# RWKV chunk in a hybrid token-mixer kernel: the key and value products ordered over all four quarters of TensorE

## The chip, the cores and the metric

One Trainium2 chip, one of its eight NeuronCores. The time is device microseconds of one execution of the whole program, which is a single launch. Before the change three runs took 4097.76, 4099.77 and 4100.25 us; the median is 4099.77 us.

## The reference

The reference is a two-layer block of a flow-matching generator over 1024 latent tokens and 256 context tokens of width 1024. Each layer normalises, projects by `w_in`, runs three groups of recurrent heads (RetNet retention, gated linear attention, RWKV-7), joins them in one output projection and ends with a SwiGLU feed-forward part. Every scan runs forward and backward. The part that matters here is the RWKV-7 scan with six heads of width 64:

```python
def _rwkv_scan(seq, s0):
    """S_t = S_{t-1}(diag(w_t) - kk_t^T (kk_t a_t)) + v_t^T k_t, o_t = S_t r_t."""
    def step(s, inp):
        rt, wt, kt, vt, kkt, at = inp
        sa = jnp.einsum("bhvk,bhk->bhv", s, -kkt)
        s = s * wt[:, :, None, :] + sa[..., None] * (kkt * at)[:, :, None, :] + vt[..., None] * kt[:, :, None, :]
        return s, jnp.einsum("bhvk,bhk->bhv", s, rt)
...
o_c, o_l = _bidirectional(_rwkv_scan, _rwkv_scan, cf, cb, lf, lb, s0)
```

## The kernel before, in words

The scan is done in chunks of 64 tokens. `rwkv` makes 20 steps in each layer, and a step holds one forward and one backward chunk (d = 0, 1). For each step `pre(u)` prepares what does not need the state and runs two steps ahead, and `step(u)` does the recurrence. In layer 0 all 20 steps give an output; in layer 1 the four context steps give none, so 36 steps of the 40 have the full set of products.

Six heads are three pairs j with two halves e: half e lies on partitions 64e to 64e+63 of `AR` (decayed queries and erase keys) and `BK` (keys). In `pre` the products of `AR` and `BK` are made by the code of lines 1282 to 1307. For half e there are first products, six matmuls 128 columns wide, whose result is masked by VectorE into `SA` (one instruction) and `SR` (two), and second products, six matmuls 64 columns wide, masked into `SR` by two more. A half's rows sit on one 64-row half of the array; the two directions d go to its two 64-column halves. So a half uses two quarters of the array, and the two halves use the other two each.

All these results go to PSUM tiles with the tag `d`, of which there are two (`self.pr("d", 2)`). The same two hold the block products of `XE` and `Wc` (32 by 32) that come just ahead in `pre`, and the transposes of `BK` that follow (line 1314, evicted to `BKT`). A tile is reused when its readers are done.

In the profile `rd` is a PSUM tile of that tag, `ra`, `rs` and `rb` are the PSUM tiles of `step`, `pd` are the dense products of the input projections of the gated linear attention and the retention (`gla_in`, `ret_in`), and `gvs`, `gkhT` are operands of the state update of the gated linear attention. Nearly all matmuls have line 245 (`mm`), since one helper issues them; the masks have line 640. An f32 matmul of the program is two matmul instructions in the trace, so six make 12.

What sets the order: the program is not run in the order of the code. `TileContext(nc, schedule_with_timeline_sim=True)` reorders the instructions of each engine by a planned timeline; `tc.high_priority` puts `step` and `pre` ahead (`HP = 5000,4500,4500`), and `run` feeds the dense products of `gla_in` and `ret_in` between the steps by a budget (`DT`, `N1`, `N2`). TensorE takes its instructions in the order so planned.

Of the kernel before, what the change touches and what calls it, by code (L numbers as in the profile page):

```python
# [16 lines left out]
D = 1024  # L17
# [21 lines left out]
SR = 0  # L39
# [131 lines left out]
class Kern:  # L171
# [287 lines left out]
    def rwkv_in(self, l, V, W1, xh, xl, ctx_out):  # L459
# [27 lines left out]
        def col(ct, wh, wl, c0, full, rows=128):  # L487
# [17 lines left out]
            c = self.t(p, [128, PW], "c", bufs=4)  # L505
            R = slice(0, rows)
            tp = V["taps"]
            self.act(c[R], u[R, 1:PW + 1], AF.Copy, scale=tp[R, 1, ct:ct + 1])
            nc.vector.scalar_tensor_tensor(c[R], u[R, 0:PW], tp[R, 0, ct:ct + 1], c[R], op0=ALU.mult, op1=ALU.add)
            nc.vector.scalar_tensor_tensor(c[R], u[R, 2:PW + 2], tp[R, 2, ct:ct + 1], c[R], op0=ALU.mult, op1=ALU.add)  # L510
            return c
# [169 lines left out]
    def rw_inverses(self, l, p):  # L681
# [3 lines left out]
        for u in range(20):  # L685
# [9 lines left out]
            for e in range(2):  # L695
                R = slice(64 * e, 64 * e + 64)
                ps = self.pn()
                for j in range(3):
                    for d in range(2):
                        a, k = M[R, d, j, 0:64], M[R, d, j, 64:128]  # L700
                        self.mm(ps[64 * d:64 * d + 64, 64 * j:64 * j + 64], *((a, k) if d else (k, a)))
# [531 lines left out]
    def rwkv(self, l, V, ctx_out):  # L1233
# [3 lines left out]
        mA, mK, mB = (self.rwmask[:, 64 * i:64 * i + 64] for i in (1, 2, 3))  # L1237
# [6 lines left out]
        D = range(2)  # L1244
        heads, masked, where = self.rw_heads, self.rw_masked, rw_where

        def pre(u):
            out = ctx_out or u >= 4
# [3 lines left out]
            AR = self.t(p, [128, 2, 3, 128], "AR", bufs=NB)  # L1252
            BK = self.t(p, [128, 2, 3, 128], "BK", bufs=2)
# [17 lines left out]
            ps = self.pr("d", 2)  # L1271
# [10 lines left out]
            SA = self.t(p, [128, 6, 64], "SA", bufs=NB)  # L1282
            SR = self.t(p, [128, 2, 6, 64], "SR", bufs=NB) if out else None
            n = 128 if out else 64
            for e in range(2):
                R = slice(64 * e, 64 * e + 64)
                ps = self.pr("d", 2)
                pv = ps[:, 0:384].rearrange("p (j x) -> p j x", j=3)
                for j in range(3):
                    for d in D:  # L1290
                        q = 64 - 64 * d
                        self.mm(pv[q:q + 64, j, 0:n], BK[R, d, j, q:q + 64], AR[R, d, j, 0:n])
                masked(heads(SA, e), pv[:, :, 0:64], mA)
                if not out:
                    continue
                for d in D:
                    q = slice(64 - 64 * d, 128 - 64 * d)
                    masked(heads(SR[q, d], e), pv[q, :, 64:128], mK[q])
                ps = self.pr("d", 2)
                pv = ps[:, 0:192].rearrange("p (j x) -> p j x", j=3)  # L1300
                for j in range(3):
                    for d in D:
                        q = 64 * d
                        self.mm(pv[q:q + 64, j], BK[R, d, j, q:q + 64], AR[R, d, j, 64:128])
                for d in D:
                    q = slice(64 * d, 64 * d + 64)
                    masked(heads(SR[q, d], e), pv[q], mB[q])
            nc.vector.tensor_tensor(BK.rearrange("p d j x -> p (d j) x"), BK.rearrange("p d j x -> p (d j) x"),
                                    PC.rearrange("p d j -> p (d j)").unsqueeze(2).to_broadcast([128, 6, 128]), op=ALU.mult)
            BKT = self.t(p, [128, 2, 384], "BKT", bufs=NB)  # L1310
            for d in D:
                ps = self.pr("d", 2)
# [67 lines left out]
        with hp(1):  # L1380
            cur = [pre(u) for u in range(2)]
        yield
        for u in range(20):
            with hp(0):
                step(u, cur[u])
            if u + 2 < 20:
                with hp(1):
                    cur.append(pre(u + 2))
            yield
# [574 lines left out]
```

## Time and profile before

| what | value |
|---|---|
| median of 3 runs | 4099.77 us |
| the profiled execution, its own time | 4102.32 us |
| its span, first to last instruction | 4100.5 us |
| granted TensorE clock, mean of the span | 0.959 |
| TensorE matmul busy | 3765.7 us, 92% of the span |
| VectorE busy | 2590.2 us, 63% |
| ScalarE busy | 1755.4 us, 43% |
| GpSimd busy | 1507.7 us, 37% |

The span and the time of the profiled execution differ by 1.8 us, which lies around the instructions; that execution was 2.5 us above the median. The page cuts the span into 40 slices of 102.5 us. The products of the change lie between 347 and about 745 us (layer 0) and between about 2495 and 2876 us (layer 1). Matmuls are pipelined: a row's length is from its start to the end of its last result, so what a group occupies on TensorE is read from its start to the start of the next group.

### The profile page before, as it was taken

How to read it: one execution, taken by the hardware profiler on the slowest of the kernel's cores; microseconds unless marked ns; L12 is line 12 of the kernel's file. 1: busy time of each engine (PE TensorE's matmuls, PEld its weight loads, DVE VectorE, ACT ScalarE, POOL GpSimd, SP SyncE). 2: the span in 40 equal slices, each digit the busy share in tenths (PEclk: the TensorE clock that was granted, in tenths of full speed). 3: DMA queues.
4: the chain of work that ended last, by engine and by line, in shares of the span. 5: the costliest groups of instructions: out<-in, count | busy, mean ns of one | idle time of the engine just before them, and what ended most of it. 6: DMA issues, size and time to landing. Idle time of an engine off the chain costs nothing. (4 is left out here: it accounts for less than half of the span.)

```text
span 4100.5 us, 78165 instructions
## 1 busy us (share of the span) xinstructions
PE 3765.7 (92%) x30344; PEld 3125.4 (76%) x30344; DVE 2590.2 (63%) x4602; ACT 1755.4 (43%) x3538; POOL 1507.7 (37%) x1670
## 2 busy tenths in 40 slices
PE   7998999889998999999994997999889988999998
PEld 4776888776677988888883675887766768999886
DVE  3565657657846766665765464667657578556666
ACT  5442334234436744443524443344234465344442
POOL 1155640333435823224331145740323443222443
PEclk9998999999999999999996998999989999999999
DMA  7487545655516522125421387555754232222542
GB/s 225 110 238 187 134 124 156 179 178 186 174 64 215 185 75 93 72 82 211 140 88 57 95 229 203 136 145 142 203 183 143 91 133 98 83 75 97 186 163 103
DMA packets 624771, 582.55 MB, mean 142 GB/s; under 512 B 315276, under 2 KB 517264, under 8 KB 607504
## 3 DMA queue, kind: packets, MB, share of 16 engines
q1 hardware_dynamic: 624112, 576.50, 46.1%
q8 instruction: 240, 3.93, 0.4%
q0 software_dynamic: 288, 1.05, 0.1%
q14 instruction: 131, 1.07, 0.1%
HBM read 431.14 MB, written 146.28 MB: 141 GB/s over the span
## 5 line engine op out<-in xcount | busy, mean ns | idle before, releaser
L1456 POOL TENSOR_TENSOR slo<-raw,shi 128x512 fp32r<-128x512 f32 x467 | 668.2, 1446 | 1084.0 <-ACT shi L1455 996.4
L1455 ACT CAST shi<-raw 128x512 fp32r<-128x512 f32 x478 | 293.7, 621 | 495.0 <-PE pd L245 199.6
L1736 DVE TENSOR_TENSOR f<-pm,f 128x512 f32<-128x512 f32 (+1 forms) x400 | 252.1, 635 | 167.9 <-PE pm L245 164.4
L245 PE MATMUL pm<-hh,shi 128*128 128x512 f32 (+1 forms) x880 | 327.7, 373 | 8.5 <-ACT hh L1722 5.3
L439 POOL TENSOR_TENSOR wlo<-wraw,whi 128x512 fp32r<-128x512 f32 x120 | 167.7, 1407 | 440.7 <-ACT whi L438 439.8
L245 PE MATMUL pm<-hl,shi 128*128 128x512 f32 (+1 forms) x880 | 326.3, 371 | 0.3 <-DVE hl L1723 0.3
L245 PE MATMUL pm<-hh,slo 128*128 128x512 f32 (+1 forms) x880 | 325.0, 369 | 0.0
L245 PE MATMUL pd<-whi,xh 128*128 128x256 f32 x1072 | 314.7, 294 | 2.7 <-DVE st L443 2.7
L245 PE MATMUL pd<-wlo,xh 128*128 128x256 f32 x1072 | 314.1, 293 | 0.5 <-POOL wlo L439 0.5
L245 PE MATMUL pd<-whi,xl 128*128 128x256 f32 x1072 | 314.0, 293 | 0.0
L245 PE MATMUL pd<-xh,whi 128*128 128x512 f32 (+1 forms) x720 | 270.8, 376 | 17.6 <-DVE xl L383 12.0
L245 PE MATMUL pd<-xl,whi 128*128 128x512 f32 (+1 forms) x720 | 272.1, 379 | 3.4 <-DVE xl L383 3.1
L245 PE MATMUL pd<-xh,wlo 128*128 128x512 f32 (+1 forms) x720 | 268.5, 373 | 0.9 <-POOL wlo L439 0.9
L1455 ACT CAST shi<-tw 128x512 fp32r<-128x512 f32 x200 | 123.5, 620 | 303.5 <-PE pd L245 230.9
L245 PEld LDWEIGHTS pd<-whi,xh 128*128 128x128 f32 x1072 | 209.5, 196 | 10.4 <-DVE st L443 3.3
L245 PEld LDWEIGHTS pd<-wlo,xh 128*128 128x128 f32 x1072 | 210.2, 196 | 7.9 <-issue 5.4
L245 PEld LDWEIGHTS pd<-whi,xl 128*128 128x128 f32 x1072 | 210.1, 196 | 6.7 <-issue 4.7
L245 PEld LDWEIGHTS pm<-hh,shi 128*128 128x128 f32 x880 | 166.2, 189 | 42.8 <-DVE f L1736 6.9
L245 PEld LDWEIGHTS pm<-hl,shi 128*128 128x128 f32 x880 | 166.7, 189 | 29.6 <-DVE hl L1723 1.4
L245 PEld LDWEIGHTS pm<-hh,slo 128*128 128x128 f32 x880 | 166.4, 189 | 28.4
L1456 DVE TENSOR_TENSOR slo<-tw,shi 128x512 fp32r<-128x512 f32 x200 | 143.5, 718 | 64.9 <-ACT shi L1455 64.8
L245 PEld LDWEIGHTS pd<-xh,whi 128*128 128x128 f32 x720 | 140.1, 195 | 49.1 <-DVE xl L383 13.5
(402 smaller groups left out, 10905.8 us busy)
## 6 DMA issues: line engine op xcount, KB each, us to landing
raw<-in_wgu SPq DMA_DIRECT2D x72, 1024.0 KB
wmod<-in_w_mod SPq DMA_DIRECT2D x192, 256.0 KB
raw<-in_wd SPq DMA_DIRECT2D x44, 1024.0 KB
wraw<-in_w_in SPq DMA_DIRECT2D x100, 256.0 KB
a<-ops SPq DMA_DIRECT2D x80, 288.0 KB
h<-h SPq DMA_DIRECT2D x44, 512.0 KB
h<-u SPq DMA_DIRECT2D x19, 1024.0 KB
X<-ops SPq DMA_DIRECT2D x36, 480.0 KB
```

What stands on the lines that cost most here:

```text
L245: return self.nc.tensor.matmul(out, l, r, start=start, stop=stop, skip_group_check=skip)
L439: nc.gpsimd.tensor_tensor(wl[i][:, :, w], r, wh[i][:, :, w].bitcast(F32), op=ALU.subtract)
L1455: self.nc.scalar.copy(hi, src)
L1456: e.tensor_tensor(lo, src, hi.bitcast(F32), op=ALU.subtract)
L1736: nc.vector.tensor_tensor(facc[b][:, m, :], ps, facc[b][:, m, :], op=ALU.add)
```

## The change: what it does

The loop over the halves e moves inside. A new inner function `halves` takes a PSUM tile of tag `d` for each half and issues, for each pair j, the products of both halves and both directions, which lie on the four 64 by 64 quarters of the array. First products of both halves are issued first, then the masks, then the second products of both halves. The numbers of matmuls, masks and PSUM tiles stay what they were.

```diff
             n = 128 if out else 64
-            for e in range(2):
-                R = slice(64 * e, 64 * e + 64)
-                ps = self.pr("d", 2)
-                pv = ps[:, 0:384].rearrange("p (j x) -> p j x", j=3)
+            E = range(2)
+
+            def halves(width, x0, swap):
+
+                pv = [self.pr("d", 2)[:, 0:3 * width].rearrange("p (j x) -> p j x", j=3) for _ in E]
                 for j in range(3):
+                    for e in E:
+                        for d in D:
+                            R, q = slice(64 * e, 64 * e + 64), 64 - 64 * d if swap else 64 * d
+                            self.mm(pv[e][q:q + 64, j, 0:width], BK[R, d, j, q:q + 64], AR[R, d, j, x0:x0 + width])
+                return pv
+            pv = halves(n, 0, True)
+            for e in E:
+                masked(heads(SA, e), pv[e][:, :, 0:64], mA)
+            if out:
+                for e in E:
                     for d in D:
-                        q = 64 - 64 * d
-                        self.mm(pv[q:q + 64, j, 0:n], BK[R, d, j, q:q + 64], AR[R, d, j, 0:n])
-                masked(heads(SA, e), pv[:, :, 0:64], mA)
-                if not out:
-                    continue
-                for d in D:
-                    q = slice(64 - 64 * d, 128 - 64 * d)
-                    masked(heads(SR[q, d], e), pv[q, :, 64:128], mK[q])
-                ps = self.pr("d", 2)
-                pv = ps[:, 0:192].rearrange("p (j x) -> p j x", j=3)
-                for j in range(3):
+                        q = slice(64 - 64 * d, 128 - 64 * d)
+                        masked(heads(SR[q, d], e), pv[e][q, :, 64:128], mK[q])
+                pv = halves(64, 64, False)
+                for e in E:
                     for d in D:
-                        q = 64 * d
-                        self.mm(pv[q:q + 64, j], BK[R, d, j, q:q + 64], AR[R, d, j, 64:128])
-                for d in D:
-                    q = slice(64 * d, 64 * d + 64)
-                    masked(heads(SR[q, d], e), pv[q], mB[q])
+                        q = slice(64 * d, 64 * d + 64)
+                        masked(heads(SR[q, d], e), pv[e][q], mB[q])
```

The planned order moves with it. On TensorE, in the third step of layer 0 (its queries are `AR_3494`, its keys `BK_3495`), this is the difference at the last products of `pre`; `ra` belongs to the recurrence of the same step, and lines with - are the order before:

```order
 L245 MATMUL pd_4175<-whi_731_3802,xl_111_316 128x256
-L245 MATMUL rd_3563<-AR_3494,BK_3495 64x128 x6
-L245 MATMUL rd_3573<-AR_3494,BK_3495 64x64 x6
 L245 MATMUL pd_4175<-whi_732_3803,xh_110_315 128x256
 L245 MATMUL pd_4175<-wlo_734_3805,xh_110_315 128x256
 L245 MATMUL pd_4175<-whi_732_3803,xl_111_316 128x256
+L245 MATMUL rd_3564<-AR_3494,BK_3495 64x64 x6
+L245 MATMUL ra_5215<-SAV_3506,SA_3542 64x64 x2
+L245 MATMUL rd_3565<-AR_3494,BK_3495 64x64 x6
+L245 MATMUL ra_5215<-SAV_3506,SA_3542 64x64 x8
+L245 MATMUL ra_5215<-SD_647_3199,AR_3494 64x128 x6
```

Before, the second half's first and second products (`rd_3563`, `rd_3573`) stood together here; now the second products of both halves (`rd_3564`, `rd_3565`) do, and the recurrence's products `ra` stand among them and behind, in one stretch.

Further up in the same step, on TensorE in the order after the change, the first products of one half (`rd_3544`) stand behind the block products `rd_3513` and six of `rs`, and those of the other half (`rd_3545`) do not follow them:

```order
L245 MATMUL rs_4044<-SD_646_3198,AR_3321 64x128 x6
L245 MATMUL rd_3513<-XE_3509 32x32 x12
L245 MATMUL rd_3544<-AR_3494,BK_3495 64x128 x6
L245 MATMUL pd_3962<-whi_731_3802,xh_108_313 128x256
L245 MATMUL pd_3962<-wlo_733_3804,xh_108_313 128x256
...
L245 MATMUL rd_3513<-Wc_3512,XE_3509 32x32
L245 MATMUL rd_3545<-AR_3494,BK_3495 64x128 x6
L245 MATMUL ra_5215<-SAV_3506,SA_3542 64x64 x2
```

The tile of `rd_3545` is the one that `rd_3513` holds until its second round is evicted, so 18 dense products and the second round of the block products lie between the two halves' first products.

One more place, on TensorE before the change, where the gated linear attention updates its state with two chunk halves in two PSUM tiles (the rows of `gvs` and `gkhT` of `pd_5480` lie on the first 64 partitions, those of `pd_5488` on the other 64):

```order
L245 MATMUL pd_5420<-whi_908_5401,xl_107_312 128x256
L245 MATMUL rd_7714<-AR_7645,BK_7646 64x128 x6
L245 MATMUL pd_5480<-gvs_5458,gkhT_5477 64x96 x4
L245 MATMUL pd_5488<-gvs_5458,gkhT_5477 64x96 x4
L245 MATMUL rd_7724<-AR_7645,BK_7646 64x64 x6
L245 MATMUL pd_5681<-whi_907_5400,xh_106_311 128x256
```

The change leaves these products as they are. All four of the one row half stand ahead of all four of the other.

## Rows read from the trace of the kernel before

**Rows 1.** The page: span, and busy time of each engine

```profile
span 4100.5 us, 78165 instructions
PE 3765.7 (92%) x30344; PEld 3125.4 (76%) x30344; DVE 2590.2 (63%) x4602; ACT 1755.4 (43%) x3538; POOL 1507.7 (37%) x1670
```

**Rows 2.** Windows: busy time in the two stretches that hold the scan

```profile
core 0: us, PE busy (x) PEld busy (x) DVE busy (x) ACT busy (x) POOL busy (x), PEclk, DMA share, GB/s
345.00:745.00 400.00, 378.58 (x5671) 327.89 (x5672) 249.29 (x574) 149.86 (x428) 151.41 (x250) 0.97 0.53 138
2495.00:2890.00 395.00, 369.92 (x5535) 318.70 (x5536) 254.96 (x563) 156.70 (x451) 169.57 (x280) 0.98 0.56 146
```

**Rows 3.** Waits of TensorE, 345 to 745 us: sum, times, longest

```profile
PE rs L245 <- ACT R L1333: 7.9, 4, 4.5
PE rd L245 <- DVE SR L640: 2.9, 4, 1.2
...
PE rd L1314 <- DVE BK L1308: 1.3, 2, 1.0
```

**Rows 4.** Waits of TensorE, 2495 to 2890 us

```profile
PE rd L245 <- DVE SR L640: 4.5, 4, 2.3
PE ra L245 <- DVE SA L640: 1.9, 2, 1.0
```

**Rows 5.** Groups by form, whole span: the products that the change orders

```profile
L245 PE MATMUL rd<-AR,BK 64*64 64x128 f32 x864 | 64.6, 282 | 3.7 <-ACT XE L1281 3.7
L245 PE MATMUL rd<-AR,BK 64*64 64x64 f32 x960 | 44.8, 224 | 7.4 <-DVE SR L640 7.4
```

**Rows 6.** Timeline of TensorE at 638 us: start, length, group

```profile
637.99 0.87 PE L245 MATMUL rd<-AR,BK 64*64 64x128 f32 x12 [1.09 <-ACT XE L1281]
638.70 0.57 PE L245 MATMUL pd<-gvs,gkhT 64*64 64x96 f32 x16
639.03 0.51 PE L245 MATMUL rd<-AR,BK 64*64 64x64 f32 x12
639.47 0.39 PE L245 MATMUL pd<-whi,xh 128*128 128x256 f32 x1
...
640.26 0.80 PE L245 MATMUL ra<-SAV,SA 64*64 64x64 f32 x20
640.99 0.88 PE L245 MATMUL ra<-SD,AR 128*64 128x128 f32 x12
```

**Rows 7.** Timeline of TensorE at 357 us

```profile
356.96 0.28 PE L245 MATMUL pd<-wlo,xh 128*128 128x256 f32 x1
357.08 0.28 PE L245 MATMUL pd<-whi,xl 128*128 128x256 f32 x1
357.29 0.87 PE L245 MATMUL rd<-AR,BK 64*64 64x128 f32 x12
359.20 0.56 PE L245 MATMUL rd<-AR,BK 64*64 64x64 f32 x12 [1.03 <-DVE SR L640]
```

**Rows 8.** Timeline of TensorE at 386 us (12 of 128 and 12 of 64 columns)

```profile
385.95 1.22 PE L245 MATMUL rd<-AR,BK 64*64 64x128 f32 x24
387.10 0.38 PE L245 MATMUL pd<-whi,xl 128*128 128x256 f32 x1
```

**Rows 9.** Timeline of VectorE at 358 us: masks behind the key products

```profile
355.09 1.44 DVE L1257 TENSOR_TENSOR BK<-X 128x192 f32<-128x192 f32 x1
356.45 1.97 DVE L1258 TENSOR_TENSOR BK<-X 128x192 f32<-128x192 f32 x1
358.34 0.71 DVE L640 TENSOR_TENSOR SR<-rd,rwmask 64x192 f32<-64x192 f32 x2
359.08 0.36 DVE L640 TENSOR_TENSOR SA<-rd,rwmask 128x192 f32<-128x192 f32 x1
359.47 0.72 DVE L640 TENSOR_TENSOR SR<-rd,rwmask 64x192 f32<-64x192 f32 x2
```

**Rows 10.** Tile SR: masks, ns min/median/max; then who waited, us, times

```profile
L640 DVE TENSOR_TENSOR SR<-rd,rwmask x288: 336/356/364, 352.4 to 2877.1; 64x192 f32<-64x192 f32 x144
...
PE rd L245: 7.4, 8
```

## The prediction

> **What bounds the kernel now.** I read the page first: matmuls are busy for 3765.7 of 4100.5 us, and no other engine comes near [rows 1]. A share over the whole span does not say what the scan is worth, so the second view was the busy time by windows around the two stretches that hold the products of the change. There TensorE is busy for 378.58 of 400 us and 369.92 of 395 us, VectorE for 249 and 255 [rows 2]. TensorE stands for 21.4 and 25.1 us, 46.5 us in both. So the scan is bound by TensorE's own work: the recurrence is covered by dense products that the planner puts between its links, and a microsecond of TensorE time saved there is a microsecond off the stage, as long as no new wait eats it. What comes after the stage is moved forward as a whole: the later parts start when this stage gives back its pools.
>
> The third view was the waits of TensorE. On the masks of `SR` it waited 2.9 us in four places in layer 0 and 4.5 us in four in layer 1 [rows 3, 4]; the tile view gives the same 7.4 us over eight [rows 10]. The largest other one here is `rs` on the copy `R`, 7.9 us [rows 3]. The key products are 864 instructions of 128 columns and 960 of 64 [rows 5]: 36 steps of 24 and 24, and four steps with 24 of 64.
>
> **What a group of products costs now.** Within a half, two quarters already work at once. The 12 instructions of 128 columns occupy TensorE from 637.99 to 638.70, 0.71 us; the 12 of 64 columns from 639.03 to 639.47, 0.44 us, with the way out to the full array [rows 6]. Without that way out the 64-column group is the difference of two rows: 24 instructions with both widths last 1.22 us [rows 8], the 12 wide ones alone 0.87 [rows 7], so 0.35 us.
>
> Do the two row halves run side by side when they stand together? The state update of the gated linear attention answers it: 16 instructions of 96 columns, eight on each row half in PSUM tiles of their own, go from 638.70 to 639.03, 0.33 us [rows 6]. At the rate of one row half (0.71 / 12 = 0.059 us for 128 columns, 0.044 for 96) they would take 16 x 0.044 = 0.71 us. So four quarters do it in half the time, although in the order all of one half stand ahead of all of the other. The order within a stretch matters little; that both halves are in one stretch matters.
>
> A rule speaks against this. The Trainium skill, "TensorE: Matmul & The Clock Gate", "Part 3: Packing small matmuls — row/col tiling", says that matmuls start and end strictly in program order and only weight loads are pulled ahead; in the section "Wait — 56ns, not 53.3ns?" it says that start-to-start never drops below about 25 ns however small the matmul. By the first, two halves that follow each other would not overlap at all and the gain on the second products would be nothing; by the second, an estimate from that page, 24 instructions of 64 columns would take at least 24 x 0.025 = 0.60 us against 0.70 now, so 0.10 us a step and not 0.35. The state update took 0.33 / 16 = 21 ns an instruction, out of order by halves; the trace disagrees with both here.
>
> **The change part by part.** Matmuls, masks, transposes and PSUM tiles keep their numbers. What moves is who stands with whom.
>
> First products (128 columns). The code issues both halves alternately, but the planned order has the two halves' first products in one stretch in 0 of 36 steps, as before: one half takes the free `d` tile, the other waits for the tile of the block products and stands 18 dense rows later. Gain 0. Were they together it would be 0.71 - 12 x 0.004 us, about 0.7 us a step, 25 us in all; that is the upper end and a rival.
>
> Second products (64 columns). Before, both halves share a stretch in 0 of 36 steps; after, in 27. Each saves one group: 27 x 0.35 = 9.5 us. Lower end 0 (no overlap), upper end 36 x 0.35 = 12.6. That the products of `ra` stand among them costs nothing: they use the same 64 by 64 shape.
>
> Changes of shape. I call a stretch a run of matmuls in the order that use the array in one tile shape. Entering a small shape from the full array costs 0.21 us from start to start where dense rows stand 0.12 apart, 0.09 more [rows 7]; leaving costs the 0.44 - 0.35 = 0.09 of above. Between small shapes: 20 instructions of `ra` take 640.26 to 640.99, 0.73 us, of which 20 x 0.35 / 12 = 0.58 is streaming, so 0.15 for way in and out together [rows 6]. I take 0.15 us a stretch. The order has 363 stretches before and 315 after from the first to the last `rd` of layer 0, and 358 and 322 in layer 1; behind layer 1's scan it has 242 and 256, and elsewhere none more or less. Net 48 + 36 - 14 = 70 fewer, 70 x 0.15 = 10.5 us. Ends: 0, if these switches lie beside waits anyway, and 70 x 0.18 = 12.6. Part of this is the planner's luck and not the change's idea: now the second products of both halves ride with `ra`.
>
> Waits. A step's masks do not change in number or price: `SA` 0.36 us, two of `SR` 0.71 [rows 9]. Before, the second half's first products needed the tile that three masks of the first half had to leave, which is the 1.03 us wait at 359.20 and the like [rows 7, 10]. After, second products need tiles that three masks a half must leave, six masks or 2.1 us in a row, and the order puts 15 to 18 dense rows (1.8 to 2.2 us at 0.12) between the second half's first products and the second products. So the old wait of 7.4 us can go, and one of the same kind can come. Behind the waiting matmul stand the second products, `ra` of the recurrence and the dense products, all of TensorE. I take 0; the ends are 7.4 us gained and 36 x 1.03 = 37 us lost.
>
> Sum: 9.5 + 10.5 = 20 us less. The profiled execution took 4102.3 us, 1.8 of it around the span; 4102.3 - 20 = 4082.3, and the median of the runs is 2.5 below that execution: 4079.8, say 4080.
>
> **The rivals.**
>
> 1. More than that: the masks' wait goes (7.4), `ra` also fits beside, and stage waits shrink: 4080 - 7.4 - 5 = 4068 and below; with the first products side by side as well 4055. For it: the halves' streams are independent in the state update. Against: 0 of 36 in the order. Chance 0.08.
>
> 2. No difference to be told: the halves do not overlap on the key products as they did on the state update (a tile's wait stands between them, or `ra` holds the queue), so 9.5 becomes 0 to 3, and half of the switches were beside waits: 4099.8 - 3 - 5 = 4092, and a microsecond or two of new waits puts it at 4093 to 4106. For it: the planner's order is new in the whole stage, and the 46.5 us that TensorE stands there [rows 2] can move by some us either way. Chance 0.20. The Trainium skill's rule of strict program order, named above, would lead here. The variant in which the change does not do what it says belongs here: it already holds for the first products.
>
> 3. Slower: the second products wait on the six masks of both tiles. VectorE is behind where its key products are long (1.44 and 1.97 us just ahead of the masks [rows 9]), and now both tiles hang on it at once, so nothing of `pre` can start. At the 1.03 us of row 359.20 in each of 36 steps this costs 37 us: 4080 + 37 = 4117. It beats the gain from the point where waits of `rd` on the masks grow by more than 20 us, so past 27 us in all against 7.4. Against it: 1.8 to 2.2 us of dense products stand ahead in most steps. Chance 0.12.
>
> **How the numbers follow.** The forecast, 4080 with its own range 4068 to 4091, has 0.60. What a measurement can tell from no change is about 0.2%, 8.2 us: faster is below 4091.6, slower above 4108.0. Faster 0.60 + 0.08 = 0.68, same 0.20, slower 0.12. The range 4060 to 4102 leaves out the far part of rival 1 (0.02), the upper part of rival 2 (0.05) and rival 3 (0.12).
>
> **What would show it.** In the profile after: groups of the key products of 64 columns keep x960 but their union of busy time falls from 44.8 us, while the 128-column ones stay near 64.6 [rows 5]; a timeline row of both halves' second products goes in about 0.35 us for 24 instructions; the stage's busy time of TensorE is 8 to 12 us less a layer, with standing time about as now. Wrong would be: 24 second products that take 0.7 us (no overlap); waits of `rd` on the masks over 20 us; or the same busy time and a shifted stage end, which would say that the stage was not bound by TensorE.

## The result, and the profile after

The changed kernel is slower: 4125.67 us median of four runs (4116.6 to 4132.05), against 4098.77 (4094.44 to 4100.25) for the kernel before on the same chip. The ratio is 1.0062, with a 95% interval of 1.0039 to 1.0085. The prediction said 4080 us; its sign is wrong. The profiled execution of the changed kernel took 4116.6 us, the lowest of its four runs, so the traces account for 14 us and the medians for 27. Most of what is missing goes with the clock: that execution had a granted clock of 0.955, the other three, of 4125.5 to 4132.1 us, 0.950 to 0.952. Over all repeated runs here a run is some 2.8 us longer where its clock is 0.001 lower than its kernel's mean (an estimate by a straight line), so 0.0035 less is worth about 10 us.

The page, span and busy times; the rows of before are [rows 1]:

```profile
span 4114.8 us, 78164 instructions
PE 3757.8 (91%) x30344; PEld 3118.0 (76%) x30344; DVE 2606.3 (63%) x4602; ACT 1757.5 (43%) x3538; POOL 1504.5 (37%) x1670
```

TensorE is busy for 7.9 us less and the span is 14.3 us longer. The windows around the two scans, against [rows 2]:

```profile
core 0: us, PE busy (x) PEld busy (x) DVE busy (x) ACT busy (x) POOL busy (x), PEclk, DMA share, GB/s
345.00:745.00 400.00, 370.11 (x5682) 323.25 (x5683) 256.57 (x573) 150.68 (x429) 152.73 (x253) 0.96 0.53 137
2495.00:2890.00 395.00, 361.37 (x5449) 313.28 (x5450) 247.36 (x554) 155.80 (x443) 167.64 (x282) 0.94 0.55 145
```

Busy time fell by 8.5 us in each window, inside the predicted 8 to 12. In windows of a fixed length standing time (time in which TensorE does nothing) then rises by as much, from 21.4 to 29.9 and from 25.1 to 33.6 us, and the second window holds 86 matmuls fewer; so the windows alone do not say what was gained. The granted clock went from 0.97 and 0.98 to 0.96 and 0.94. The groups by form over the whole span, against [rows 5]:

```profile
L245 PE MATMUL rd<-AR,BK 64*64 64x128 f32 x864 | 63.7, 279 | 3.5 <-DVE SR L640 3.4
...
L245 PE MATMUL ra<-SAV,SA 64*64 64x64 f32 x960 | 51.8, 230 | 13.7 <-DVE SA L640 12.8
...
L245 PE MATMUL rd<-AR,BK 64*64 64x64 f32 x960 | 42.3, 235 | 3.7 <-ACT XE L1281 3.6
```

The busy time of the 64-column products fell from 44.8 to 42.3 us only, less than the sign that the prediction gave. Their instructions now stand among those of `ra`, and such rows overlap; what they occupy is read from starts, below. The wait of `rd` on the masks of `SR`, which rival 3 was about, fell from 7.4 to 3.4 us. TensorE waits elsewhere now: first the rows for 345 to 745 us, then those for 2495 to 2890 us (sum, times, longest), against [rows 3, 4]:

```profile
PE rs L245 <- ACT R L1334: 10.9, 8, 4.0
PE ra L245 <- DVE SA L640: 7.9, 5, 2.8
...
PE rd L245 <- DVE SR L640: 0.4, 2, 0.2
```

```profile
PE rs L245 <- ACT R L1334: 13.5, 4, 7.4
...
PE ra L245 <- DVE SA L640: 4.9, 7, 1.8
PE rd L245 <- DVE SR L640: 3.0, 7, 0.5
```

Before, TensorE did not wait for `SA` in layer 0, and for `R` in layer 1 only this long:

```profile
PE rs L245 <- ACT R L1333: 1.6, 3, 1.0
```

So the waits for `R` went from 9.5 to 24.4 us, those for `SA` from 1.9 to 12.8, those for `SR` from 7.4 to 3.4: 21.8 us more.

The overlap of the two halves is seen at 537.74 us on TensorE's timeline:

```profile
537.74 0.57 PE L245 MATMUL rd<-AR,BK 64*64 64x64 f32 x22
538.24 0.38 PE L245 MATMUL pd<-xh,whi 128*128 128x256 f32 x1
```

22 of the 24 instructions of both halves' second products occupy TensorE for 0.50 us; 12 of one half alone took 0.44 with the way out [rows 6]. So the four quarters do work side by side. The Trainium skill, "TensorE: Matmul & The Clock Gate", in "Wait — 56ns, not 53.3ns?", has a floor of about 25 ns from start to start; here it is 0.50 / 22 = 23 ns with the way out included, and the measurement decides.

**Where the time went, stretch by stretch.** I cut the two layers where the scan begins (first `rd`), where it ends (last product of `step`) and where the last dense product of the input projections stands. Before, then after, scan and rest in turn for layer 0 and layer 1:

```profile
346.60:745.50 398.90, 378.41 (x5676) 328.16 (x5678) 247.69 (x572) 149.86 (x428) 149.97 (x248) 0.97 0.52 138
745.50:880.80 135.30, 112.68 (x907) 106.65 (x903) 77.25 (x198) 31.39 (x75) 46.54 (x52) 0.91 0.62 180
2515.20:2885.80 370.60, 353.03 (x5401) 304.70 (x5403) 242.83 (x537) 146.39 (x421) 149.38 (x245) 0.99 0.56 145
2885.80:2994.20 108.40, 91.72 (x758) 87.23 (x754) 68.63 (x178) 23.27 (x56) 46.13 (x59) 0.97 0.70 204
```

```profile
346.00:741.60 395.60, 367.19 (x5648) 320.83 (x5650) 254.49 (x568) 149.93 (x427) 151.81 (x252) 0.96 0.52 137
741.60:876.00 134.40, 116.06 (x934) 109.27 (x931) 79.30 (x202) 30.81 (x76) 45.05 (x50) 0.90 0.64 186
2516.10:2891.60 375.50, 348.07 (x5367) 302.25 (x5367) 236.28 (x533) 148.35 (x419) 148.81 (x246) 0.96 0.55 142
2891.60:3011.60 120.00, 97.86 (x792) 92.08 (x788) 71.61 (x183) 24.11 (x58) 46.84 (x57) 0.91 0.65 190
```

Layer 0 gains 3.3 us in the scan and 0.9 behind it. Layer 1 loses 4.9 us in its scan although TensorE is busy for 5.0 us less, and 11.6 us behind it, at a clock of 0.91 instead of 0.97. Together that is 12.3 of the 14.3 us.

**A sum that closes.** For the rest I divide a span into three parts: standing time (span less TensorE's busy time); what half clock cost, estimated as half of the time in which TensorE was busy while the trace's clock record shows the lower of its two levels, 1.2 instead of 2.4 GHz; and the remainder, which I call work. Before: 4100.5 = 3663.4 work + 334.8 standing + 102.3 half clock. After: 4114.8 = 3645.1 + 356.9 + 112.8. The change is -18.3 + 22.1 + 10.5 = +14.3. Nearly all of the predicted 20 us of work did go. It was paid for by standing time and clock.

The work can be split further: it is the sum, over TensorE's instructions, of the time from each start to the next start, with half clock taken off. The 64-column key products take 27.2 us of it, against 36.9 before, so 9.7 of the 18.3 us are theirs. The other 8.6 us lie on other rows, 7.0 of them on `rb`. There the trace has fewer changes of shape: 1342 runs of one tile shape in the whole span against 1412.

Standing time and half clock are seen in one place. ScalarE and TensorE in layer 1's scan after the change:

```profile
2612.21 0.62 ACT L438 CAST whi<-wraw 128x512 fp32r<-128x512 f32 x1 [6.81 <-DMA wraw<-in_w_in]
2612.74 0.47 ACT L1334 COPY R<-ra 128x384 f32<-128x384 f32 x1
```

```profile
2613.26 1.55 PE L245 MATMUL rs<-R,XE 64*64 64x64 f32 x24 [5.47 <-ACT R L1334]
```

The copy of `R`, which the recurrence needs, stands in ScalarE's queue behind a cast that waits 6.81 us for its load; TensorE stands for 5.47 us. The same happens 100 us later with 7.39 us. The windows around three long waits between 2600 and 2915 us (the third is 5.01 us, of `pd` on `gz`, behind the scan) show the clock:

```profile
2611.00:2618.00 7.00, 4.74 (x41) 4.62 (x42) 0.47 (x2) 2.31 (x8) 6.45 (x12) 0.53 0.87 237
2618.00:2640.00 22.00, 19.94 (x304) 18.07 (x304) 16.66 (x35) 9.34 (x31) 19.65 (x31) 1.00 0.46 122
2690.00:2710.00 20.00, 16.37 (x189) 13.26 (x181) 8.73 (x17) 5.32 (x15) 17.80 (x31) 0.99 0.43 120
2710.00:2720.00 10.00, 5.79 (x44) 5.67 (x45) 2.11 (x6) 2.74 (x8) 3.06 (x3) 0.50 0.85 187
2720.00:2740.00 20.00, 20.00 (x310) 18.39 (x309) 12.80 (x34) 10.51 (x28) 1.28 (x1) 1.00 0.44 123
...
2901.00:2915.00 14.00, 8.42 (x42) 7.53 (x43) 8.24 (x18) 2.83 (x7) 6.75 (x8) 0.52 0.87 260
```

The clock is full ahead of a wait and for 20 us afterwards, and half (0.50 to 0.53) at the end of the wait and over the matmuls just after it. So a long wait costs more than its own length. The Trainium skill says the same in "TensorE: Matmul & The Clock Gate", "HAM oscillation — how this bites in real kernels": gaps bring the clock down and the next matmuls pay. These rows agree.

Half clock also comes without such a wait. Later in the same scan:

```profile
2836.00:2846.00 10.00, 9.75 (x176) 8.22 (x175) 7.86 (x22) 5.14 (x15) 0.20 (x1) 1.00 0.50 131
2846.00:2857.00 11.00, 10.60 (x124) 9.02 (x125) 5.03 (x14) 2.92 (x10) 0.00 (x0) 0.53 0.44 140
```

TensorE was busy for 9.75 of the 10 us ahead, the last 6 of them with the small products of the scan and hardly a dense one; its longest wait there was 0.52 us.

### The profile page after: what moved, and what is told of

It is laid out like the page before. It is cut to its first block, busy times and chain, and to the rows that moved or that the text cites. A ratio compares the mean times of both kernels' runs of the same rounds, so it can differ in the third digit from the quotient of the medians.

```text
span 4114.8 us, 78164 instructions
## 1 busy us (share of the span) xinstructions
PE 3757.8 (91%) x30344; PEld 3118.0 (76%) x30344; DVE 2606.3 (63%) x4602; ACT 1757.5 (43%) x3538; POOL 1504.5 (37%) x1670
## 5 line engine op out<-in xcount | busy, mean ns | idle before, releaser
L245 PEld LDWEIGHTS pd<-whi,xh 128*128 128x128 f32 x1072 | 212.5, 199 | 12.8 <-issue 5.9
L725 POOL TENSOR_TENSOR L<-L,itmp 96x30 f32<-96x30 f32 (+5 forms) x300 | 168.9, 563 | 22.5
```

Source lines behind the costliest of these rows:

```text
L245: return self.nc.tensor.matmul(out, l, r, start=start, stop=stop, skip_group_check=skip)
L725: eng.tensor_tensor(L3[:, 0:u, u + 1:32], L3[:, 0:u, u + 1:32], t3, op=ALU.subtract)
```

## The experiments

Eighteen kernels ran besides the two of the change; the two without a planned order are told of at their place. Ratios are to the kernel before, run beside them on the same chip. The parts of the sum are those of each kernel's profiled execution, worked out as above; "together" says whether second products of both halves share stretches.

| kernel | together | ratio [95%] | span | work | standing | half clock |
|---|---|---|---|---|---|---|
| before | no | 1 | 4100.5 | 3663.4 | 334.8 | 102.3 |
| after | yes | 1.0062 [1.0039, 1.0085] | 4114.8 | 3645.1 | 356.9 | 112.8 |
| second_only | yes | 1.0044 [1.0024, 1.0064] | 4129.5 | 3645.5 | 355.9 | 128.1 |
| first_only | yes | 1.0000 [0.9983, 1.0016] | 4106.1 | 3648.7 | 346.6 | 110.8 |
| rev | no | 0.9993 [0.9978, 1.0007] | 4100.1 | 3653.9 | 334.2 | 112.1 |
| after_edge | yes | 1.0103 [1.0080, 1.0127] | 4150.5 | 3635.0 | 369.8 | 145.6 |
| before_rdve | no | 1.0024 [1.0010, 1.0038] | 4112.7 | 3662.4 | 338.3 | 112.0 |
| after_rdve | yes | 1.0038 [1.0025, 1.0051] | 4121.0 | 3639.5 | 351.0 | 130.5 |
| before_poolcast | no | 1.0030 [1.0012, 1.0048] | 4102.2 | 3661.4 | 336.0 | 104.7 |
| after_poolcast | yes | 1.0010 [1.0000, 1.0020] | 4096.5 | 3639.4 | 334.3 | 122.8 |
| after_sav3 | yes | 1.0013 [1.0000, 1.0026] | 4106.2 | 3647.5 | 336.1 | 122.7 |
| before_xb2 | no | 1.0003 [0.9988, 1.0018] | 4111.1 | 3661.2 | 326.4 | 123.5 |
| rev_xb2 | no | 1.0005 [0.9987, 1.0023] | 4101.1 | 3654.8 | 333.4 | 112.9 |
| after_xb2 | yes | 0.9963 [0.9948, 0.9979] | 4078.9 | 3646.0 | 325.3 | 107.6 |
| after_poolcast_xb2 | yes | 0.9988 [0.9972, 1.0004] | 4106.3 | 3647.0 | 336.9 | 122.3 |
| first_only_xb2 | yes | 1.0059 [1.0036, 1.0082] | 4112.5 | 3641.0 | 337.7 | 133.8 |
| before_less | left out | 1.0020 [1.0001, 1.0038] | 4105.5 | 3625.8 | 354.8 | 124.9 |
| before_twice | no | 1.0159 [1.0136, 1.0182] | 4160.0 | 3689.1 | 341.0 | 129.9 |

A profiled execution is one of the runs and can lie some 10 us off the kernel's median (after_xb2: 4078.9, median 4093.4), so the parts are read across kernels, the verdicts from the ratios. Half clock scatters most: over the runs of the kernel before alone the granted clock goes from 0.954 to 0.962, 33 us of the span's clock (an estimate, 0.008 of 4100 us).

### Which part of the change does it: second_only, first_only, rev

Second products together, first products half by half as before:

```diff
-            pv = halves(n, 0, True)
             for e in E:
-                masked(heads(SA, e), pv[e][:, :, 0:64], mA)
+                pv = halves(n, 0, True, range(e, e + 1))
+                masked(heads(SA, e), pv[0][:, :, 0:64], mA)
```

> The second products of both halves together, the first products half by half as before. Theory ScalarE queue (the new plan lets the copy of R stand behind instructions that wait for loads: 22 of 40 against 6 of 40 before, in this kernel again 22): as the changed kernel, 4115 to 4135 us. Theory tiles (both PSUM tiles hang on one block of six masks): as the changed kernel or some us better, 4100 to 4130. If the interleaved first products were the cost: 4075 to 4095.

4121.6 us, 1.0044: the loss is there with the second products alone. Only TensorE's order differs from that of the changed kernel, and only nearby; ScalarE, GpSimd and SyncE run in the same order. So its trace is nearly a second trace of the same program: work and standing time agree within 1 us, and its span is 14.7 us longer by half clock alone (128.1 against 112.8). Differences of that size in the last column need not come from the kernel. The first products' interleaving is inert, as predicted; the planned order had kept them apart in any case.

First products in one loop, second products half by half in the code:

```diff
-                pv = halves(64, 64, False)
                 for e in E:
+                    pv = halves(64, 64, False, range(e, e + 1))
```

> The first products of both halves issued together, then the masks, then the second products half by half. The planned order still has the second products in one stretch in 29 of 36 steps, and the copy of R behind a load's consumer in 16 of 40. Theory ScalarE queue: between, 4095 to 4120 us. Theory tiles: the second products need one tile at a time, so 4080 to 4100.

4108.6 us, 1.0000. The planned order brings the second products of both halves together all the same (29 of 36 steps), so this is another plan of the same work and not the first products alone. It has the work of the changed kernel, 3648.7, and about half of the added standing time (+11.8 against +22.1 us).

The kernel before with the halves in the other order, for a new plan without the change:

```diff
-            for e in range(2):
+            for e in (1, 0):
```

> The kernel before with its loop over the halves run in the other order (1, 0): the same work, a new plan, no sharing of quarters, copy of R behind a load's consumer in 5 of 40. Theory ScalarE queue: as before or some us faster through fewer changes of shape, 4085 to 4105 us. Theory that any new plan costs (the order before was a lucky one): 4110 to 4135.

4101.2 us, 0.9993: this new plan is not a loss. It is also worth something for the sum: its halves share no stretch and its 64-column key products take 38.8 us, no less than the 36.9 before, but it has 1367 runs of one shape instead of 1412, and 9.5 us less work. So about half of what the change took off TensorE can be had from an order without the four quarters.

### Is it the place of the copy of R: after_edge, before_rdve, after_rdve

In the planned order of ScalarE the copy of `R` stands directly behind the consumer of a load (the cast `whi`, or one of the exponentials `P` and `X<-X` of a step's loaded operands; an expectation below calls the second one the square of `X`) in 6 of 40 steps before and in 22 after. In `after_edge` the casts and activations issued after a step's copy of `R` are held behind it:

```diff
-                    nc.scalar.copy(wh[i][:, :, w], r)
+                    self.behind(nc.scalar.copy(wh[i][:, :, w], r))
...
-            self.act(P[:, d, :, 1:65], cu, AF.Exp, scale=-half)
+            self.behind(self.act(P[:, d, :, 1:65], cu, AF.Exp, scale=-half))
...
-            nc.scalar.copy(R0, pa[:, 0:384])
+            self.rcopy = nc.scalar.copy(R0, pa[:, 0:384])
```

> The changed kernel with an order (no wait) on ScalarE: the decay activations P and the weight casts whi that the code emits after a step's copy of R also stand behind it. Theory ScalarE queue: the gain shows, 4070 to 4095 us, waits of rs on R under 10 us in all. Theory tiles, or any new plan costs: 4110 to 4135.

4150.2 us, 1.0103, the slowest of the versions with the change, outside what either theory gave. The wait for `R` falls to 0.4 us in layer 0 and 5.0 in layer 1, and the time does not come back. TensorE's longest waits at 345 to 745 us:

```profile
PE rd L250 <- DMA XE<-xe: 9.6, 1, 9.6
PE ra L250 <- DVE SA L645: 7.7, 5, 2.1
```

The 9.6 us are one wait, from 336.1 to 345.7 us, ahead of the scan's first product and of the first copy of `R` at 353.4 us, so nothing that was held behind a copy can have made it; in the changed kernel TensorE stood for 2.1 us there. Layer 1 has the like, 8.8 us. This is again another plan, and it leaves open what the copy's place costs by itself. In the next pair the copy of `R` runs on VectorE, in either kernel:

```diff
-            nc.scalar.copy(R0, pa[:, 0:384])
+            nc.vector.tensor_copy(R0, pa[:, 0:384])
```

> The kernel before with the copy of R on VectorE, where no instruction waits for a load directly. Theory ScalarE queue: the 9.5 us of waits of rs on R go, 4085 to 4100. Theory supply: no difference, 4090 to 4110.

> The changed kernel with the copy of R on VectorE (both halves' second products in one stretch in 21 of 36). Theory ScalarE queue: the 24.4 us of waits of rs on R go and the gain shows, 4075 to 4095. Theory supply: the waits move elsewhere (ra on SA, rd on XE, rb on BKT), 4100 to 4130.

4114.1 and 4120.6 us, 1.0024 and 1.0038. The wait for `R` falls from 10.9 to 2.1 us in the first scan, and two others take its place, so the theory of the ScalarE queue misses in both kernels (`after_rdve`, 345 to 745 us):

```profile
PE rs L245 <- DVE SAV L1340: 8.2, 3, 4.9
PE ra L245 <- DVE SA L640: 6.2, 4, 2.4
...
PE rs L245 <- DVE R L1334: 2.1, 1, 2.1
```

### Is it what feeds ScalarE: poolcast, sav3

The casts of the input projections' weights on GpSimd, so that nothing on ScalarE waits for `wraw`; in both kernels:

```diff
-                    nc.scalar.copy(wh[i][:, :, w], r)
+                    (nc.gpsimd.tensor_copy if width == 256 else nc.scalar.copy)(wh[i][:, :, w], r)
```

> The kernel before with the casts of the input projections' weights (whi<-wraw, 256 wide) on GpSimd instead of ScalarE. It is the other half of the pair with the changed kernel. ScalarE loses some 40 casts of about 0.4 us a scan, which the copy of R seldom stood behind here. Theory of the in-order queue of ScalarE: 0.998 to 1.003 of the kernel before, 4097 to 4117 us. Rival (GpSimd is late with the casts, and the dense products wait for them): 1.004 and above, 4120 us and more.

> The changed kernel with the casts whi<-wraw (256 wide) on GpSimd instead of ScalarE. In the changed kernel the copy of R stands directly behind such a cast in 7 of 40 steps, and the two longest waits of TensorE for R in layer 1 (5.5 and 7.4 us) came just behind casts that waited for their load; with the casts elsewhere no copy of R stands behind one. Theory A (the wait for R behind a cast that waits for its load costs the second scan its time): waits for R in layer 1 fall from 13.5 us to under 5, and the kernel comes to 0.998 to 1.002 of the kernel before (4097 to 4113 us). Theory B (the loads themselves are late, above all that of X with its one buffer, and the wait shows wherever the next consumer stands): waits for R fall, others take their place, and the time stays at 1.003 to 1.008 (4117 to 4138 us).

4113.7 us (1.0030) and 4102.4 us (1.0010). (ScalarE has 20 such casts of 0.62 us in the first scan of the kernel before, not some 40 of 0.4 us.) The same edit makes the kernel before slower and the loss is gone from the changed one: with it the change is a gain of 11.3 us on `before_poolcast`. Waits for `R` in layer 1's scan fall from 13.5 to 4.4 us and standing time over the span by 22.6:

```profile
PE ra L245 <- DVE SA L640: 7.4, 7, 2.5
PE rs L245 <- ACT R L1334: 4.4, 5, 2.9
```

Theory A of the expectation (the wait behind the cast) has both its wait and its time right, and theory B misses; half clock stays high, at 122.8. That the moved casts are the reason is not shown by this alone, since the next version leaves them on ScalarE and has nearly no loss either.

Three buffers of `SAV` and `XE`, the other tiles that SyncE loads for each step:

```diff
-            SAV = self.t(p, [128, 2, 384], "SAV", bufs=NB)
+            SAV = self.t(p, [128, 2, 384], "SAV", bufs=3)
...
-            XE = self.t(p, [128, 6, 128], "XE", bufs=NB)
+            XE = self.t(p, [128, 6, 128], "XE", bufs=3)
```

> The changed kernel with three buffers instead of two of SAV and XE, the other two tiles that SyncE loads for every step; X keeps its one buffer. Theory X (the one buffer of X is what keeps the changed kernel from using the time freed on TensorE): no gain from this, 1.003 to 1.008 of the kernel before, 4117 to 4138 us at a kernel before of 4105. Rival S (SyncE's queue as a whole is held up by loads that wait for a buffer to come free, whichever it is): 0.995 to 1.000, 4085 to 4105 us, and the waits of SyncE's queue for TensorE's rs shrink by half or more.

4105.2 us, 1.0013. Theory X (the buffer of `X` alone) wanted 1.003 and more and misses. Rival S wanted 1.000 or less and the waits of SyncE's queue for `rs` halved; they are 41.3 us in the first scan against 46.1, so its mechanism is not shown either. Standing time fell by 20.8 us, and the waits for `R` from 24.4 to 11.8.

### Is it the one buffer of X: the four with XB = 2, and the plan

```diff
-XB = 1
+XB = 2
```

> The kernel before with two buffers for X, the loaded operands of a step, in place of one: a step's loads no longer wait until the readers of the step before are done. Theory supply (a step's loads and the in-order queues behind them set the pace of the scan, so TensorE time saved turns into standing time): 4075 to 4095 us, waits of P on X<-ops fall below half of 82.7 us. Theory ScalarE queue alone: as before, 4090 to 4110. Theory any new plan costs: 4105 to 4130.

> The changed kernel with two buffers for X. The planned order has both halves' second products in one stretch in 34 of 36 steps, and the copy of R behind a load's consumer in 16 of 40 (before_xb2: 2). Theory supply: the change shows its TensorE gain now, 10 to 20 us under before_xb2, 4060 to 4080. Theory ScalarE queue (place of the copy of R): still slower than before_xb2, 4090 to 4115. Theory tiles (both PSUM tiles on six masks): 4100 to 4125, waits of ra on SA as in the changed kernel.

4105.6 us (1.0003) and 4093.4 us (0.9963). ScalarE's wait for `X`, 82.7 us in the first scan of the kernel before, leaves the head of the list in both, and the kernel before gains nothing by it, against the theory of supply. The changed kernel becomes the fastest of all, 12.2 us below `before_xb2`, as that theory said, though 13 us above its range: of the change's 15.2 us of work most is kept, as in the pair with the moved casts. I took this for the cause, and tried it on other plans.

> The kernel before with the loop over the halves turned round (second half first) and two buffers of X instead of one. The halves stay apart: no products of the two halves share a stretch. It asks whether the gain of the version with two buffers of X and the products of both halves together came from the four quarters or from any new order together with the second buffer. Theory (the four quarters take about 8 us of each scan off TensorE, and the second buffer of X lets the stage use it): no gain here, 0.998 to 1.003 of the kernel before, that is 4097 to 4117 us at a kernel before of 4105. Rival (a new order with two buffers of X is what paid): 0.994 to 0.997, 4080 to 4093 us.

> The first products of both halves in one loop, the second products half by half in the code, two buffers of X. In the planned order the second products of both halves share a stretch in 20 of 36 steps (34 in the version of the changed kernel with two buffers of X). Account 1 (two buffers of X let the scan use the time freed): 0.995 to 0.998 of the kernel before, 4082 to 4094 us at a kernel before of 4102. Account 2 (plans scatter): anywhere from 0.998 to 1.006, 4094 to 4127 us.

> The changed kernel with two buffers of X and the casts whi<-wraw on GpSimd. No copy of R stands behind such a cast, 2 of 40 stand behind the square of X; the second products share a stretch in 20 of 36 steps. With one buffer of X the move of the casts brought the changed kernel from 1.006 to 1.001 and the kernel before from 1.000 to 1.003. Account 1: 0.994 to 0.998 of the kernel before, 4078 to 4094 us. Account 2: 0.998 to 1.006, 4094 to 4127 us.

`rev_xb2` 4101.4 us (1.0005): without the four quarters nothing is gained. But `first_only_xb2` took 4123.3 us (1.0059) and `after_poolcast_xb2` 4099.6 (0.9988), with the second products together in 20 of 36 steps each. Account 1 falls with the first of them: two buffers of `X` do not make the change pay in general. Its loss is the clock: work 3641.0, standing 337.7, half clock 133.8. The one plan that is faster than the kernel before clear of the noise is `after_xb2`.

Without the planned timeline:

```diff
-    with tile.TileContext(nc, schedule_with_timeline_sim=True) as tc:
+    with tile.TileContext(nc) as tc:
```

> The kernel before without the planned timeline (the engines take the instructions in the order in which the program issues them by its priorities). The halves share a stretch of second products in 25 of 36 steps even here, by the order of the code. It is the base of the pair: slower than the planned kernel, 1.02 to 1.15, 4184 to 4717 us, by either account.

> The changed kernel without the planned timeline. The first products of both halves share a stretch in 28 of 36 steps (2 in the unplanned kernel before), the second products in 30 (25). If TensorE's own work sets the pace where no plan stands between, it is 0.995 to 0.998 of the unplanned kernel before (28 steps of first products at about 0.7 us a scan pair, some 10 to 20 us); if the waits set it, within 0.2% of it or slower.

4583.0 us (1.1171 [1.1154, 1.1187]) and 4577.0 (1.1154 [1.1133, 1.1175]). The intervals overlap: 6 us between them are not told from nothing, although the first products of both halves share a stretch in 28 of 36 steps here. In the trace they do not run side by side: at 498.31 us all 12 of one half start by 498.92, the 12 of the other from 499.12, and the 24 occupy TensorE for 1.50 us. So the 25 us that the prediction names for the first products stay untested. By the sum above the changed kernel has 12.8 us more work here, 17.2 us more standing time and 53.6 us less half clock; the saving in work is seen in planned orders alone.

### The premise by itself: before_less, before_twice

The kernel before with its second products left out (the masks read the first products instead), and with them issued twice:

```diff
-                ps = self.pr("d", 2)
-                pv = ps[:, 0:192].rearrange("p (j x) -> p j x", j=3)
-                for j in range(3):
-                    for d in D:
-                        q = 64 * d
-                        self.mm(pv[q:q + 64, j], BK[R, d, j, q:q + 64], AR[R, d, j, 64:128])
                 for d in D:
                     q = slice(64 * d, 64 * d + 64)
-                    masked(heads(SR[q, d], e), pv[q], mB[q])
+                    masked(heads(SR[q, d], e), pv[q, :, 64:128], mB[q])
```

```diff
-                for j in range(3):
+                for j in [0, 1, 2] * 2:
```

> The kernel before without the second products: their masks read the first products' tile instead, so SR has other values; the masks, copies and loads stay. It takes 72 groups of 12 instructions off TensorE, 0.35 to 0.5 us each (25 to 36 us), and the planned order has 50 and 44 stretches of one shape fewer in the two scans (at 0.15 us 14 us): 39 to 50 us of TensorE's time. Premise of the prediction (TensorE's own work sets the pace of the scan): 0.988 to 0.991 of the kernel before, 4053 to 4065 us at a kernel before of 4104. Rival (the time freed turns into standing time and half clock): at most half of it comes off, 0.994 to 1.002, 4080 to 4112 us.

> The kernel before with the second products issued twice (the second time over the first result, with the same values). It puts 72 groups of 12 instructions of 64 columns on TensorE, 0.3 to 0.35 us each where they follow their like, some 21 to 25 us, and 20 more stretches in the planned order (3 us). Premise (TensorE's own work sets the pace): 1.006 to 1.007, 4128 to 4133 us. Rival (other waits set it, and standing time takes the work in): at most half, 1.000 to 1.003, 4104 to 4116 us.

4111.0 us (1.0020) and 4165.8 us (1.0159). Leaving out twice what the change could save gained nothing. In the sum: work -37.6 (39 to 50 expected), standing +20.0, half clock +22.6. Issuing it twice cost far more than its own time: work +25.7 (24 to 28 expected), standing +6.2, half clock +27.6. Neither number fits the premise, and the second does not fit the rival either. The windows of `before_less`, scan and rest in turn as above:

```profile
347.90:703.40 355.50, 334.37 (x5020) 291.17 (x5022) 250.10 (x546) 138.76 (x411) 152.07 (x248) 0.98 0.56 147
703.40:869.50 166.10, 139.19 (x1082) 128.89 (x1079) 81.48 (x224) 37.33 (x92) 46.23 (x53) 0.87 0.57 163
2509.40:2853.10 343.70, 321.56 (x4824) 277.98 (x4823) 230.03 (x509) 136.30 (x401) 148.85 (x242) 0.97 0.57 148
2853.10:3005.50 152.40, 122.23 (x957) 112.16 (x954) 76.47 (x208) 32.47 (x78) 46.31 (x63) 0.85 0.58 166
```

The scans are 43.4 and 26.9 us shorter, and the rests 30.8 and 44.0 us longer. Some 175 and 199 matmuls that ran between the steps now stand behind the scan, where TensorE stands for 27 and 30 us and runs at a clock of 0.87 and 0.85 instead of 0.91 and 0.97. Scan and rest together, layer 0 gains 12.6 us and layer 1 loses 17.1. In the changed kernel the same can be seen in small: 27 and 34 matmuls more behind the scan, and 11.6 us more in layer 1.

## Why the prediction was wrong, point by point

- **First products, gain 0:** right. `second_only` leaves them as before and has the same loss.
- **Second products on four quarters, 9.5 us, and 70 fewer changes of shape, 10.5 us:** right in mechanism and nearly in size. The 64-column products take 9.7 us less, and 70 fewer runs of one shape go with 8.6 us less on other rows, together 18.3. The second half is not the change's idea: `rev` has 9.5 us less work with the halves apart. That 24 second products would go in 0.35 us was a little too short: 22 took 0.50 with the way out, 0.41 without the 0.09 that the prediction gives it. Every version with the second products together has 3635 to 3649 us of work, every one with them apart, `before_twice` aside, 3654 to 3663.
- **Waits, taken as 0, ends 7.4 gained and 37 lost:** this is the term that failed in the sum. It measured +22.1 us of standing time, inside its range. The place was wrong: not the masks of `SR` (7.4 to 3.4 us), but the copy of `R` (9.5 to 24.4) and the masks of `SA` (1.9 to 12.8), which the recurrence needs. I looked at the tile that the change touches and not at what else stands in the queues of ScalarE once the plan is new. The order would have shown it: 22 of 40 copies of `R` directly behind the consumer of a load, against 6.
- **A term that was not there:** half clock, +10.5 us in the traces, a difference that one trace alone does not prove, and by the clocks more in the median run (0.9515, the trace 0.955); up to 43 in other versions. The rows of before had the clock at 0.97 and 0.98 [rows 2], and I took it as given. The kernel before has the highest clock of all planned kernels, 0.957 to 0.958 in the median of its runs against 0.9455 to 0.9565, so any other order had something to lose.
- **The premise "a microsecond of TensorE time saved there is a microsecond off the stage, as long as no new wait eats it", and "what comes after the stage is moved forward as a whole":** this is the step that failed and decided the sign. `before_less` is the counterexample: 37.6 us of TensorE's work less, and the kernel 1.0020 of before, with 20.0 us more standing time and 22.6 us more half clock. I concluded the premise from a high busy share. In that stretch the busy time is partly dense products that fill the steps: when a step gets shorter they are pushed behind the scan, where little covers their waits.
- **Rivals:** rival 3 had the sign and the size (4117; measured 4125.67), but its mechanism, waits of `rd` on the masks, did not happen. Rival 2 had the reason in half a sentence (the standing time can move with the new plan) and only a microsecond or two for it; its other reason, that the halves would not overlap, did not come: 22 instructions in 0.50 us. In rival 1 the figure 4055 is 4080 less 25 and leaves out the 12 us that stand just before it; with them it is 4043.

What is shown: the work went nearly as predicted, standing time and half clock took its place, and the copy of `R` behind casts that wait for loads is one place of it in layer 1. The loss belongs to the plan and not to the four quarters: `first_only`, `after_poolcast` and `after_sav3` share them and are within 0.13% of the kernel before. That the copy behind the casts is what cost the time is argued, not shown: moving the casts away goes with no loss, and so does leaving them with three buffers of `SAV` and `XE`. What stays open: why one plan of the same work keeps the gain (0.9963) and another of nearly the same work does not (1.0059). No count that I made of the order foretells it, neither the steps together nor the places of the copy; over the ten versions with the second products together the ratio goes from 0.9963 to 1.0103, over the six with them apart and no work added from 0.9993 to 1.0030.

The fastest version found is the changed kernel with two buffers of `X`, 4093.4 us, ratio 0.9963 [0.9948, 0.9979].

## What to carry to other kernels

A high busy share of an engine in a stage is no proof that work taken off it shortens the program: leave the work out altogether once and time that, before the cheaper form of it is priced, and read the stretch behind the stage too, where the work may have gone. In a planned order a new shape of the work is a new order of every queue, so read on the other engines what the critical copies stand behind, and count a wait of several us with the half clock that comes with it. Judge such a change over several plans of it, since one plan's time can lie half a per cent from another's with the same work.

## What the hardware showed that was not expected

- The time in which TensorE is at half clock moves with the order of the work as much as the work does: from 337 us of the span before to 409 us in `first_only_xb2` and 469 us in `after_edge`, with the same matmuls. The kernel before alone goes from about 310 to 380 us over its runs (an estimate from their clocks, 0.962 to 0.954).
- TensorE went to half clock after a wait of 5 to 7 us, and also, at 2846 us of the changed kernel, out of 10 us in which it was busy for 9.75, the last 6 with small products.
- Adding work can cost over twice its own time, here in one plan: 25.7 us of extra second products made the span 59.5 us longer, 27.6 of it by half clock.
- Matmuls on the two row halves run as two streams: 22 instructions of 64 columns, both halves alternating, at 23 ns each; before, 16 of 96 columns with one half wholly ahead of the other at 21 ns [rows 6].
